# One-hot rows for eight tokens, score blocks around a staging buffer, weights two units per transfer

## The chip, the cores and the metric

The kernel runs on one core of a Trainium2 chip. The metric is the device time of one execution in microseconds (us), as the median of several runs. The engines are TensorE (PE; its weight loads are PEld), VectorE (DVE), ScalarE (ACT), GpSimd (POOL) and SyncE (SP), which only issues transfers here. Transfers are issued by SyncE, ScalarE and GpSimd and run on 16 DMA engines.

## What is computed

One decoder layer for 512 tokens of width 2048: latent attention (8 heads) and a recurrent branch side by side, an output projection, and a product-key expert layer. The last takes most of the time: 16384 experts, of which each token uses 128 (8 heads, 16 each).

```python
def chunk(xc):
    q = (xc @ w_q).reshape(TOKEN_CHUNK, N_PEER_HEADS, 2, PEER_HALF)
    s1 = jnp.einsum('chd,hnd->chn', q[:, :, 0], keys1)
    s2 = jnp.einsum('chd,hnd->chn', q[:, :, 1], keys2)
    v1, i1 = lax.top_k(s1, PEER_TOPK)
    v2, i2 = lax.top_k(s2, PEER_TOPK)
    ...
    e = i1[...] * N_KEYS + i2[...]
    g = jax.nn.softmax(top, axis=-1)
    act = gelu(einsum('chk,cd->chk', u_tab[e], xc))
    return jnp.einsum('chk,chkd->cd', g * act, v_tab[e])
```

## The kernel before

**Experts, dense and gathered.** For 384 of the 512 tokens the kernel doesn't gather: it multiplies the tokens with all 16384 expert rows, in 128 score blocks (S, 128 experts each), applies GELU, multiplies with a gate that is zero for experts not chosen, and multiplies with the value table in 128 output jobs (V). For the other 128 tokens it gathers rows: `gather` (L803) issues an indirect transfer of 1 MB on GpSimd's queue, `side` (L813) works on one gathered row with VectorE, 256 times in all.

**Weights.** Every matrix product of weights is made of three (`mm3`, L160), with each float32 operand split into a high and a low part. The weights come in units of 128x1024 (512 KB), in one fixed `order` (L77 to L103) of 631 units. `emit_next` (L117) takes the next unit: it picks a pool with fewer than two units in use, issues the transfer into `raw` (L126, two buffers per pool) on SyncE, and has ScalarE make `hi` (L130) and VectorE `lo` (L131), two buffers each. `need` (L135) gives back the unit used last and calls `emit_next` until no pool has room. A pool `base` is always open; a second one is open beside it in the input projections, the second half of the output projection and the expert layer (`open_extra`, L146), and not in the attention stage between.

**The gate stage.** When the top-k is done, the gates have to be made for 384 tokens. `onehots` (L839) builds, for four tokens at a time, one-hot rows in bf16 on VectorE: two comparisons (L847, L848) and three products with the gate's three bf16 parts (L850), three buffers of the results. `gate_mm` (L855) multiplies them on TensorE into one PSUM bank (12 products, L863), ScalarE copies the bank into `stg` (L865), which has one buffer for 32 tokens, and after eight calls the store to `GD` (L868) is issued on ScalarE's queue, 2 MB. Between the calls `park` (L665) computes score blocks ahead of their turn: two units of `ud`, 48 products, a GELU on ScalarE (L674) and a store to `AD`. 44 blocks are parked in all, 10 of them in the top-k before, 32 in the loop at L872, 2 after it (L880).

```python
    for q in range(NB4):
        if q % 3 == 0:
            park()
            if q % 6 == 3 or q > 42:
                side(rowp)
        if q + 2 < NB4:
            onehots(q + 2)
        gate_mm(q)
    while parked[0] < PARK:
        park()
```

**The main loop** (L937) runs the other 84 score blocks and the 128 output jobs. It needs two units per job, loads gates for four blocks at a time with `gates` (L893, from `GD`), multiplies them in `gated` (L900), and runs `side` at a fixed rate per unit.

**What sets the order.** PSUM has eight banks; `bank()` (L60) hands them out in turn before the main loop, which has two for S and six for V. Up to L889 a planner orders each engine's instructions when the kernel is built, by their place in the source, their dependencies and its own estimates of their durations, so an engine's queue need not stand as written. From L890 on (`manual_schedule`) each engine runs in the order of the source. Each queue works in order: an instruction that waits holds up what stands behind it, SyncE's transfers included.

## Time and profile before

| what | value |
|---|---|
| median of 3 runs | 3113.37 us (3109.54 to 3116.7) |
| the profiled execution | 3107.04 us, its span 3104.9 us |
| granted TensorE clock, mean | 0.986 |
| TensorE busy | 3043.2 us |
| VectorE / ScalarE / GpSimd busy | 2284.7 / 1096.5 / 393.9 us |
| moved by DMA | 691.13 MB, 223 GB/s |

The profile is of one execution. Times within it are us from the first instruction of the span. An engine's busy time counts its instructions from start to end; those of TensorE overlap one another, so the distance between starts tells more than the duration of one. The granted clock is the share of the full clock (2.4 GHz) that TensorE was given. An idle time is put down to the instruction or transfer whose end released the next one.

### The profile page before, as it was taken

What the parts mean: (1) busy time and instruction counts of PE and PEld (TensorE: products, weight loads), DVE (VectorE), ACT (ScalarE), POOL (GpSimd) and SP (SyncE); (2) the same over time, 40 slices, a digit from 0 to 9 for tenths busy, and PEclk for the clock granted to TensorE, in tenths of its full rate; (3) what the DMA queues carried; (4) which work ended last, traced back from release to release, by engine and by line L of the source; (5) the groups of instructions that cost most, each with busy time, mean ns of one, the idle gap of its engine ahead of it and who ended that gap; (6) DMA issues with size and microseconds to landing.
All of it is one profiled execution on the core that took longest, in us unless ns stands there. A gap on an engine that the chain in (4) does not pass through costs nothing.

```text
span 3104.9 us, 39324 instructions
## 1 busy us (share of the span) xinstructions
PE 3043.2 (98%) x15443; PEld 2630.8 (85%) x15443; DVE 2284.7 (74%) x3456; ACT 1096.5 (35%) x1371; POOL 393.9 (13%) x280
## 2 busy tenths in 40 slices
PE   8999999999999999999999999999999999999999
PEld 7777565678899998999999999999999999888887
DVE  4465544448999888757777777777777777788887
ACT  4455332342234444443333333333333333333332
POOL 0000000000000011001212112122211212211111
PEclk9999898999999999999999999999999999999999
DMA  7222211232245887678787787877878778878876
GB/s 247 87 78 75 88 55 41 88 108 83 89 129 195 269 274 255 200 264 290 278 296 284 283 301 274 299 284 281 296 281 296 285 282 292 298 277 295 290 283 234
DMA packets 247306, 691.13 MB, mean 223 GB/s; under 512 B 17040, under 2 KB 128272, under 8 KB 213456
## 3 DMA queue, kind: packets, MB, share of 16 engines
q1 hardware_dynamic: 152832, 382.15, 36.8%
q0 software_dynamic: 37008, 269.50, 23.2%
q10 hardware_dynamic: 57280, 36.97, 3.9%
q8 instruction: 121, 1.98, 0.3%
q14 instruction: 65, 0.53, 0.0%
HBM read 650.40 MB, written 38.14 MB: 222 GB/s over the span
## 4 chain that ended last, share of the span: by engine, by line
PE 57%; issue 0%; DVE 0%; ACT 0%
PE pV L984 11%; PE pV L983 11%; PE pV L982 11%; PE pS L161 8%; PE pS L163 8%; PE pS L162 8%; PE ps L161 0%; PE ps L162 0%; PE ps L163 0%; PE ps L863 0%; DVE acc L996 0%; ACT pact L674 0%; DVE o L850 0%; ACT hi L130 0%
## 5 line engine op out<-in xcount | busy, mean ns | idle before, releaser
L130 ACT ACTIVATE hi<-raw 128x1024 fp32r<-128x1024 f32 x631 | 667.8, 1061 | 1489.4 <-PE pS L162 487.6
L131 DVE TENSOR_TENSOR lo<-raw,hi 128x1024 fp32r<-128x1024 f32 x631 | 771.1, 1222 | 495.2 <-ACT hi L130 481.6
L161 PE MATMUL pS<-FH,hi 128*128 128x384 f32 x1344 | 449.9, 335 | 1.3 <-ACT pact L674 1.3
L163 PE MATMUL pS<-FH,lo 128*128 128x384 f32 x1344 | 450.0, 335 | 0.0
L162 PE MATMUL pS<-FL,hi 128*128 128x384 f32 x1344 | 449.5, 334 | 0.0
L984 PE MATMUL pV<-hi,FL 128*128 128x512 f32 x960 | 374.7, 390 | 0.0
L983 PE MATMUL pV<-lo,FH 128*128 128x512 f32 x960 | 374.7, 390 | 0.0
L982 PE MATMUL pV<-hi,FH 128*128 128x512 f32 x960 | 373.4, 389 | 0.0
L161 PE MATMUL ps<-FH,hi 128*128 128x384 f32 (+1 forms) x960 | 342.8, 357 | 0.3 <-ACT hi L130 0.3
L809 POOL DMA_INDIRECT row<-in_un,E x128 | 175.6, 1372 | 1319.3 <-DVE row L821 819.3
L163 PE MATMUL ps<-FH,lo 128*128 128x384 f32 (+1 forms) x960 | 337.8, 352 | 0.6 <-DVE lo L131 0.6
L162 PE MATMUL ps<-FL,hi 128*128 128x384 f32 (+1 forms) x960 | 338.1, 352 | 0.0
L821 DVE SCALAR_TENSOR_TENSOR row<-row,xg 128x2048 f32<-128x2048 f32 x128 | 292.5, 2285 | 22.0 <-DMA row<-in_un,E 22.0
L826 DVE SCALAR_TENSOR_TENSOR acc<-row,W,acc 128x2048 f32<-128x2048 f32 x128 | 300.2, 2345 | 0.0
L809 POOL DMA_INDIRECT row<-in_vn,E x128 | 192.4, 1503 | 804.8 <-DVE acc L826 754.0
L161 PEld LDWEIGHTS pS<-FH,hi 128*128 128x128 f32 x1344 | 252.3, 188 | 4.7 <-ACT pact L674 1.7
L162 PEld LDWEIGHTS pS<-FL,hi 128*128 128x128 f32 x1344 | 252.3, 188 | 3.1
L163 PEld LDWEIGHTS pS<-FH,lo 128*128 128x128 f32 x1344 | 252.2, 188 | 0.0
L996 DVE TENSOR_TENSOR acc<-pV,acc 128x512 f32<-128x512 f32 x384 | 240.9, 682 | 8.3 <-PE pV L984 8.3
L984 PE MATMUL pV<-hi,pl 128*128 128x512 f32 x576 | 224.4, 390 | 0.0
L983 PE MATMUL pV<-lo,ph 128*128 128x512 f32 x576 | 224.2, 389 | 0.0
L982 PE MATMUL pV<-hi,ph 128*128 128x512 f32 x576 | 224.0, 389 | 0.0
(281 smaller groups left out, 4423.2 us busy)
## 6 DMA issues: line engine op xcount, KB each, us to landing
raw<-in_ud SPq DMA_DIRECT2D x256, 512.0 KB
raw<-in_vd SPq DMA_DIRECT2D x256, 512.0 KB
G<-GD SPq DMA_DIRECT2D x33, 768.0 KB
GD<-stg ACTq DMA_DIRECT2D x12, 2048.0 KB
raw<-in_win SPq DMA_DIRECT2D x44, 512.0 KB
raw<-in_wo SPq DMA_DIRECT2D x32, 512.0 KB
raw<-in_wq SPq DMA_DIRECT2D x32, 512.0 KB
AD<-pact ACTq DMA_DIRECT2D x44, 192.0 KB
```

The source lines that it names most:

```text
L130: s.activation(hi, raw, AF.Copy)
L131: v.tensor_tensor(lo, raw, hi.bitcast(F32), op=OP.subtract)
L161: pe.matmul(out, ah, bh, start=start, stop=False)
L162: pe.matmul(out, ah, bl, start=False, stop=False)
L163: pe.matmul(out, al, bh, start=False, stop=stop)
L809: g.indirect_dma_start(out=r, out_offset=None, in_=d["un" if j < 128 else "vn"], in_offset=bass.IndirectOffsetOnAxis(ap=E0[:, j % 128:j % ...
L821: v.scalar_tensor_tensor(r, r, 1.0, xg, op0=OP.mult, op1=OP.mult, accum_out=dots[:, j:j + 1])
L826: v.scalar_tensor_tensor(acc[:, 0, :], r, W0[:, j - 128:j - 127], acc[:, 0, :], op0=OP.mult, op1=OP.add)
L982: pe.matmul(pss[t], ph[:, t, :], hi[:, cs], start=pr + bj == 0, stop=False)
L983: pe.matmul(pss[t], ph[:, t, :], lo[:, cs], start=False, stop=False)
L984: pe.matmul(pss[t], pl[:, t, :], hi[:, cs], start=False, stop=pr + bj == 2)
L996: v.tensor_tensor(a, pss[t], a, op=OP.add)
```

## The change

It has four parts. The one-hot rows are built for eight tokens at a time, in half as many instructions of twice the length, with two buffers instead of three; one comparison is written into the third of the product rows, so its own buffer is gone. The loop of the gate stage has 48 steps of eight tokens; a score block is parked in three of every four steps, not in the fourth, at whose end the staging buffer is stored, and `side` runs in every second step. The weights are moved by `bring`, two units in one transfer of 1 MB into one buffer of 128x2048 per pool (the first two units, `wkr`, `wv`, `wuq` and `wuk` alone, 512 KB each), and split by `split`, one unit at a time; the tables are laid out so that both units of a pair stand in one row of 8 KB per partition. `ones`, `identb` and `maskb` move to a pool that is closed after the output projection.

```diff
-    ones = cp.tile([128, 128], F32, name="ones")
-    v.memset(ones, 1.0)
-    identb = cp.tile([128, 128], BF, name="identb")
-    maskb = cp.tile([128, 128], BF, name="maskb")
...
-    order = []
+
+    groups = []
     for m in range(6):
-        order += [("win", m, 0), ("win", m, 1)]
-    order.append(("wkr",))
+        if m == 0:
+            groups += [([("win", 0, u)], d["win"][0][:, u]) for u in range(2)]
+        else:
+            groups.append(([("win", m, 0), ("win", m, 1)], d["win"][m]))
+    groups.append(([("wkr",)], d["wkr"]))
...
     for hb in range(2):
-        order += [("wv", hb)] + [("wuq", hb, u) for u in range(3)] + [("wuk", hb)]
-        order += [("wo", dc, 4 + u) for dc in (2 * hb, 2 * hb + 1) for u in range(4)]
...
+        groups.append(([("wv", hb)], d["wv"][hb]))
+        groups += [([("wuq", hb, u)], d["wuq"][hb, u]) for u in range(3)]
+        groups.append(([("wuk", hb)], d["wuk"][hb]))
+        groups += wo_pairs(2 * hb, 4) + wo_pairs(2 * hb + 1, 4)
...
+    groups += [([("wq", m, 0), ("wq", m, 1)], d["wq"][m]) for m in range(16)]
...
         if j[0] == "S":
-            order += [("ud", j[1], 0), ("ud", j[1], 1)]
+            groups.append(([("ud", j[1], 0), ("ud", j[1], 1)], d["ud"][j[1]]))
         else:
-            order += [("vd", j[1], j[2], 0), ("vd", j[1], j[2], 1)]
+            groups.append(([("vd", j[1], j[2], 0), ("vd", j[1], j[2], 1)], d["vd"][j[1], j[2]]))
+    order = [k for keys, _ in groups for k in keys]
     pools = [base]
-    live = {id(base): 0}
+    live, busy = {id(base): 0}, {id(base): False}
     limit = [0]
+    moved, raws = [0, 0], []
     ready, nxt, used, last = {}, [0], [0], [None]
...
-    def emit_next():
+    def bring():
+
+        if moved[0] >= len(groups):
+            return False
+        keys, src = groups[moved[0]]
+        ps = pools if moved[1] + len(keys) <= limit[0] else pools[:1]
+        ps = [p for p in ps if not busy[id(p)]]
+        if not ps:
+            return False
+        p = ps[0]
+        moved[0] += 1
+        moved[1] += len(keys)
+        busy[id(p)] = True
+        raw = p.tile([128, 2048], F32, name="raw", bufs=1)[:, :len(keys) * 1024]
+        sy.dma_start(raw, src if len(keys) == 1 else src.rearrange("p u c -> p (u c)"))
+        raws.append([raw, p, len(keys), 0])
+        return True
+
+    def split():
+
         ps = pools if nxt[0] < limit[0] else pools[:1]
         ps = [p for p in ps if live[id(p)] < 2]
-        if nxt[0] >= len(order) or not ps:
+        if not raws or not ps:
             return False
-        key = order[nxt[0]]
-        nxt[0] += 1
+        r = raws[0]
+        raw = r[0][:, r[3] * 1024:(r[3] + 1) * 1024]
+        r[3] += 1
         p = min(ps, key=lambda p: live[id(p)])
         live[id(p)] += 1
-        raw = p.tile([128, 1024], F32, name="raw", bufs=2)
-        sy.dma_start(raw, unit_src(key))
         hi = p.tile([128, 1024], F32R, name="hi", bufs=2)
         lo = p.tile([128, 1024], F32R, name="lo", bufs=2)
         s.activation(hi, raw, AF.Copy)
         v.tensor_tensor(lo, raw, hi.bitcast(F32), op=OP.subtract)
-        ready[key] = (hi, lo, p)
+        ready[order[nxt[0]]] = (hi, lo, p)
+        nxt[0] += 1
+        if r[3] == r[2]:
+            raws.pop(0)
+            busy[id(r[1])] = False
         return True
+
+    def emit_next():
+        a = bring()
+        return split() or a
...
     sqB = MBp.tile([128, S], F32, name="sqB")
+    ones = MBp.tile([128, 128], F32, name="ones")
+    v.memset(ones, 1.0)
+    identb = MBp.tile([128, 128], BF, name="identb")
+    maskb = MBp.tile([128, 128], BF, name="maskb")
...
-    NT = 4
-    NB4 = TD // NT
+    NT = 8
+    NB8 = TD // NT
...
-        o2 = gp.tile([128, NT, 64, 2], BF, name="o2", bufs=3)
-        o1 = gp.tile([128, NT, 64, 2], BF, name="o1", bufs=1)
-        o3 = gp.tile([128, 3, NT, 64, 2], BF, name="o3", bufs=3)
+        o2 = gp.tile([128, NT, 64, 2], BF, name="o2", bufs=2)
+        o3 = gp.tile([128, 3, NT, 64, 2], BF, name="o3", bufs=2)
...
-        v.tensor_tensor(o1, io, e1T[:, c, None].to_broadcast(sh), op=OP.is_equal)
+        v.tensor_tensor(o3[:, 2], io, e1T[:, c, None].to_broadcast(sh), op=OP.is_equal)
         for j in range(3):
-            v.tensor_tensor(o3[:, j], o1, g3T[:, j, c, None].to_broadcast(sh), op=OP.mult)
+            v.tensor_tensor(o3[:, j], o3[:, 2], g3T[:, j, c, None].to_broadcast(sh), op=OP.mult)
...
     def gate_mm(q):
-
         o2, o1 = oh.pop(q)
-        if q % 8 == 0:
+        if q % 4 == 0:
             stg[0] = gp.tile([128, 128, 32], F32, name="stg", bufs=1)
...
+        for hf in range(2):
+            ps = bank()
+            for i in range(4):
+                for j in range(3):
+                    pe.matmul(ps[:, i * 128:(i + 1) * 128], o2[:, 4 * hf + i], o1[:, j, 4 * hf + i],
+                              start=j == 0, stop=j == 2)
+            c = (q % 4) * 8 + hf * 4
+            s.activation(stg[0][:, :, c:c + 4].rearrange("p a t -> p t a"),
+                         ps.rearrange("p (t a) -> p t a", t=4), AF.Copy)
+        if q % 4 == 3:
+            s.dma_start(GD[q // 4].rearrange("g p x -> p g x"), stg[0].rearrange("p (g a) t -> p g (a t)", a=GRP))
+
+    onehots(0)
+    for q in range(NB8):
+        if q % 4 != 3:
             park()
-            if q % 6 == 3 or q > 42:
-                side(rowp)
-        if q + 2 < NB4:
-            onehots(q + 2)
+        if q % 2 == 1:
+            side(rowp)
+        if q + 1 < NB8:
+            onehots(q + 1)
         gate_mm(q)
...
-    o["ud"] = c(o["un"].reshape(128, 128, 2, 8, 128).transpose(0, 2, 4, 3, 1)).reshape(128, 2, 128, 1024)
-    o["vd"] = c(o["vn"].reshape(32, 2, 2, 128, 4, 512).transpose(0, 4, 1, 3, 2, 5)).reshape(32, 4, 2, 128, 1024)
+    o["ud"] = c(o["un"].reshape(128, 128, 2, 8, 128).transpose(0, 4, 2, 3, 1)).reshape(128, 128, 2, 1024)
+    o["vd"] = c(o["vn"].reshape(32, 2, 2, 128, 4, 512).transpose(0, 4, 3, 1, 2, 5)).reshape(32, 4, 128, 2, 1024)
```

## Rows read from the trace of the kernel before

**Rows 1.** The page, part 1: busy us (share of the span) and instructions.

```profile
PE 3043.2 (98%) x15443; PEld 2630.8 (85%) x15443; DVE 2284.7 (74%) x3456; ACT 1096.5 (35%) x1371; POOL 393.9 (13%) x280
```

**Rows 2.** By stage: us, PE, PEld, DVE, ACT, POOL busy, clock, DMA, GB/s.

```profile
0.00:50.00 50.00, 41.05 (x166) 32.59 (x167) 26.83 (x58) 29.43 (x41) 0.43 (x5) 1.00 0.88 303
...
255.00:590.00 335.00, 324.45 (x1209) 202.89 (x1207) 169.35 (x287) 126.45 (x214) 14.91 (x11) 0.93 0.21 65
...
962.00:1351.00 389.00, 363.15 (x2789) 354.51 (x2788) 303.24 (x604) 178.10 (x203) 31.81 (x26) 0.97 0.74 242
1351.00:3105.00 1754.00, 1748.78 (x8640) 1565.46 (x8640) 1381.20 (x1398) 541.79 (x633) 336.79 (x231) 1.00 0.80 286
```

**Rows 3.** TensorE in order of time, gate stage: start, us, instruction [idle before <-releaser].

```profile
962.21 0.42 PE L161 MATMUL ps<-FH,hi 128*128 128x384 f32 x1
...
1123.13 0.42 PE L161 MATMUL ps<-FH,hi 128*128 128x384 f32 x1
...
1131.54 0.23 PE L863 MATMUL ps<-o,o 128*128 128x128 bf16 x1
...
1133.54 0.42 PE L161 MATMUL ps<-FH,hi 128*128 128x384 f32 x1
...
1148.74 0.27 PE L863 MATMUL ps<-o,o 128*128 128x128 bf16 x1 [5.28 <-ACT stg L865]
...
1150.30 0.67 PE L161 MATMUL ps<-FH,hi 128*128 128x384 f32 x1
...
1350.85 0.44 PE L161 MATMUL pS<-FH,hi 128*128 128x384 f32 x1 [1.35 <-ACT pact L674]
```

**Rows 4.** ScalarE in order of time, one store of the staging buffer.

```profile
1123.62 0.38 ACTq L868 DMA_DIRECT2D GD<-stg  x1
...
1139.43 2.10 ACT L865 ACTIVATE stg<-ps 128x512 f32<-128x512 f32 x2 [10.97 <-DMA GD<-stg]
```

**Rows 5.** The waits of all engines: us in total, times, longest us.

```profile
ACT stg L865 <- DMA GD<-stg: 61.7, 11, 11.0
...
DVE row L821 <- DMA row<-in_un,E: 22.0, 14, 3.8
...
PE ps L863 <- ACT stg L865: 12.3, 3, 5.3
...
PE ps L863 <- DVE o L850: 11.4, 4, 4.3
```

**Rows 6.** Ten us of the gate stage (columns of rows 2).

```profile
1240.00:1250.00 10.00, 6.46 (x29) 6.20 (x30) 9.73 (x22) 5.29 (x7) 0.00 (x0) 0.66 0.83 275
```

**Rows 7.** The costliest groups, shapes apart: xcount | busy us, mean ns.

```profile
L131 DVE TENSOR_TENSOR lo<-raw,hi 128x1024 fp32r<-128x1024 f32 x631 | 771.1, 1222 | 495.2 <-ACT hi L130 481.6 <-PE ps L691 8.4 <-PE ps L228 4.2
...
L821 DVE SCALAR_TENSOR_TENSOR row<-row,xg 128x2048 f32<-128x2048 f32 x128 | 292.5, 2285 | 22.0 <-DMA row<-in_un,E 22.0
...
L850 DVE TENSOR_TENSOR o<-o,g3T 128x512 bf16<-128x512 bf16 x288 | 105.1, 420 | 0.4
...
L776 DVE TENSOR_TENSOR eq<-eq 128x1024 bf16<-128x1024 bf16 x8 | 5.5, 683 | 0.0
```

**Rows 8.** The waits of SyncE's queue.

```profile
SPq L895 <- DMA GD<-stg: 11.7, 1, 11.7
```

**Rows 9.** Gathers (line 809), then the raw weights from 1400 us on.

```profile
DMA to landing us min/median/max: 5.4/7.3/10.7
...
  DMA raw<-in_vd: 12.3, 10
```

**Rows 10.** ScalarE in order of time, two units of the attention stage.

```profile
460.09 1.06 ACT L130 ACTIVATE hi<-raw 128x1024 fp32r<-128x1024 f32 x1 [2.30 <-PE ps L162]
...
467.90 1.06 ACT L130 ACTIVATE hi<-raw 128x1024 fp32r<-128x1024 f32 x1 [2.29 <-PE ps L162]
```

**Rows 11.** The start, in order of time: SyncE's queue, VectorE.

```profile
2.60 0.44 SPq L127 DMA_DIRECT2D raw<-in_win  x1
...
8.15 1.22 DVE L131 TENSOR_TENSOR lo<-raw,hi 128x1024 fp32r<-128x1024 f32 x1
```

More of the change, by code (lines that the diff above doesn't have):

```diff
@@ L66, in body, with wo_pairs @@
     ident = cst[:, K_ID:K_ID + 128]
-    ones = cp.tile([128, 128], F32, name="ones")
-    v.memset(ones, 1.0)
-    identb = cp.tile([128, 128], BF, name="identb")
-    maskb = cp.tile([128, 128], BF, name="maskb")
     def col(c):
         return vec[:, c:c + 1]
-    order = []
+    groups = []
     for m in range(6):
-        order += [("win", m, 0), ("win", m, 1)]
-    order.append(("wkr",))
+        if m == 0:
[3 more added lines that the diff above has]
+    groups.append(([("wkr",)], d["wkr"]))
     for h in range(8):
-        order += [("win", 6 + h, 0), ("win", 6 + h, 1), ("win", 14 + h, 0), ("win", 14 + h, 1)]
+        groups += [([("win", m, 0), ("win", m, 1)], d["win"][m]) for m in (6 + h, 14 + h)]
+    def wo_pairs(dc, lo_):
+        return [([("wo", dc, u), ("wo", dc, u + 1)], d["wo"][dc, u // 2]) for u in (lo_, lo_ + 2)]
     for hb in range(2):
-        order += [("wv", hb)] + [("wuq", hb, u) for u in range(3)] + [("wuk", hb)]
-        order += [("wo", dc, 4 + u) for dc in (2 * hb, 2 * hb + 1) for u in range(4)]
-    order += [("wo", dc, u) for dc in range(4) for u in range(4)]
-    order += [("wq", m, 0, u) for m in range(16) for u in range(2)]
-    order = [(k[0], k[1], k[3]) if k[0] == "wq" else k for k in order]
+        groups.append(([("wv", hb)], d["wv"][hb]))
+        groups += [([("wuq", hb, u)], d["wuq"][hb, u]) for u in range(3)]
+        groups.append(([("wuk", hb)], d["wuk"][hb]))
+        groups += wo_pairs(2 * hb, 4) + wo_pairs(2 * hb + 1, 4)
+    for dc in range(4):
+        groups += wo_pairs(dc, 0)
+    groups += [([("wq", m, 0), ("wq", m, 1)], d["wq"][m]) for m in range(16)]
     JOBS = [("S", b) for b in range(PARK)]
@@ L148, in open_extra @@
         pools.append(p)
-        live[id(p)] = 0
+        live[id(p)], busy[id(p)] = 0, False
         limit[0] = order.index(until) if until else len(order)
@@ L154, in close_extra @@
         pools.remove(p)
-        assert all(r[2] is not p for r in ready.values())
+        assert all(r[2] is not p for r in ready.values()) and all(r[1] is not p for r in raws)
         if last[0] is p:
@@ L857, in gate_mm @@
         o2, o1 = oh.pop(q)
-        if q % 8 == 0:
+        if q % 4 == 0:
             stg[0] = gp.tile([128, 128, 32], F32, name="stg", bufs=1)
-        ps = bank()
-        for i in range(4):
-            for j in range(3):
-                pe.matmul(ps[:, i * 128:(i + 1) * 128], o2[:, i], o1[:, j, i], start=j == 0, stop=j == 2)
-        qq = q % 8
-        s.activation(stg[0][:, :, qq * 4:(qq + 1) * 4].rearrange("p a t -> p t a"),
-                     ps.rearrange("p (t a) -> p t a", t=4), AF.Copy)
-        if qq == 7:
-            s.dma_start(GD[q // 8].rearrange("g p x -> p g x"), stg[0].rearrange("p (g a) t -> p g (a t)", a=GRP))
-    for q in range(2):
-        onehots(q)
-    for q in range(NB4):
-        if q % 3 == 0:
+        for hf in range(2):
[12 more added lines that the diff above has]
+        if q % 4 != 3:
             park()
-            if q % 6 == 3 or q > 42:
-                side(rowp)
-        if q + 2 < NB4:
-            onehots(q + 2)
+        if q % 2 == 1:
+            side(rowp)
+        if q + 1 < NB8:
+            onehots(q + 1)
         gate_mm(q)
@@ L1032, in layout @@
     o["wg"] = c(wg.reshape(4, 4, 128, 128).transpose(2, 0, 1, 3))
-    o["wo"] = c(a["w_out"][0].reshape(8, 2, 128, 4, 512).transpose(3, 0, 2, 1, 4)).reshape(4, 8, 128, 1024)
+    o["wo"] = c(a["w_out"][0].reshape(8, 2, 128, 4, 512).transpose(3, 0, 2, 1, 4).reshape(4, 4, 2, 128, 1024).transpose(0, 1, 3, 2, 4))
     o["wq"] = c(a["peer_w_q"][0].reshape(2, 8, 128, 16, 128).transpose(3, 2, 0, 1, 4)).reshape(16, 128, 2, 1024)
```

7 lines of the change are left out of this document (removed).

## The prediction

> **What bounds the kernel now.** I read the page's busy shares first, then the same by stage, then TensorE's own order of time in the one stage that stands out, and last what its gaps wait for. TensorE is busy 98% of the span [rows 1], so only time in which it stands still, or runs at its lower clock, can be won; the change adds and removes no matrix product. The table by stage says where such time is [rows 2]. From 1351 us on it is 1748.8 busy of 1754: nothing to win there, only to lose. The gate stage, 962 to 1351, has 25.9 us of idle time and a granted clock of 0.97; the attention stage 10.6 us at 0.93, in small products that the change leaves alone; the first 50 us have 9, before anything has landed.
>
> In the gate stage the order of time shows one repeating step [rows 3]: a score block of 48 products (1123.13 to 1131.54, 8.41 us) and then the gate products of three sets of four tokens, 36 of them in 2.00 us, so 0.056 us each; 10.41 us in all. The stage has 34 blocks and 1152 gate products (384 tokens, three each): 34 x 8.41 + 1152 x 0.056 = 350 us, where 1350.85 - 962.21 = 388.6 were taken. 38.6 us are lost. One step shows how: it begins at 1133.54 and the next at 1150.30, 16.76 us instead of 10.41, with a gap of 5.28 us that ScalarE's copy into the staging buffer ends. That copy stood still because the buffer was still being written out: the store went out at 1123.62 and the next copy began at 1139.43, after 10.97 us of waiting [rows 4], and the splits of the weights (hi) stand behind it on ScalarE. In all ScalarE waits 61.7 us for the store, eleven times; TensorE's gaps are put down to the copies (12.3 us) and to the one-hot rows (11.4 us) [rows 5], and the latter are late for the same cause, since on VectorE they stand behind a split (lo) that needs hi. After a gap the clock falls: 0.66 granted in 1240 to 1250, so of its two levels, 1.2 and 2.4 GHz, it had the lower for a part of that time [rows 6]. This is why 38.6 us are lost where 25.9 are idle.
>
> **The change part by part.** *Score blocks around the staging buffer.* The 350 us of products stay. Now each run of 32 tokens is block, 8 tokens, block, 8 tokens, block, 16 tokens, and then the store. So behind every store there is a block, 24 gate products (1.3 us) and a second block before a third bank pair is wanted: at least 18.1 us of products whose weights are split already or are split before the copy that waits. The store seen took 15.8 us from issue to next copy [rows 4]. The first copy is due a block and half a set (9.1) after the last set's products, the store itself goes out about a copy (1.0) after them, so ScalarE waits 15.8 - 8.1 = 7.7 us where it waited 11, and the splits held up behind it are for a block that starts only at 18. In PSUM two 2-bank sets and two score banks fill 6 of the 8 banks by then. So I take the gaps as gone, except for what is unknown: a slow gather (VectorE stood 22.0 us on rows in fourteen places [rows 5]) or another order of the engine queues than the source has, since a planner sets it there. Bounds 0 and 15 us (0.4 of what is lost now); I take 4, near the lower end because the margin exceeds the store shown.
>
> *One-hot rows for eight tokens.* 96 x 5 instructions of 512 columns become 48 x 5 of 1024. The rows: 420 ns for 512, 683 ns for 1024 columns of the same type [rows 7]. 480 x 0.42 = 202 us become 240 x 0.683 = 164, 38 us less on VectorE. It is worth nothing directly, as VectorE is 303 of 389 busy [rows 2]; it is cover. But a batch now takes 5 x 0.683 = 3.4 us and only two are held, so batch q+1 can start only when the products of q-1 are done. While blocks stand between the products (8.41 us) that is hidden: 3.4 us + two lo splits of 1.22 + half a side step (2.29) = 7.0 us. Between the two sets that follow one another at the end of 32 tokens the second batch was made during the block. The row says so far: hidden. A rule stands against it: the Trainium skill, Perfetto Trace Analysis, section Optimizing Scalar/DVE Operations, says that where Vector isn't saturated and causes bubbles elsewhere, instructions should be broken up, not merged. By it the batch would be waited for once in every 32 tokens; that is the first rival below. The trace agrees in so far as VectorE isn't saturated and 11.4 us of bubbles bear its name [rows 5].
>
> *The tail of the stage.* 34 blocks are used up in the twelfth run, so the last three sets have no block beside them, and the two blocks that followed the last products are gone as cover. There batch 46 waits for products 44 and takes 3.4 us less 1.5 covered by products 45: 1.9 us idle, and the same for 47: 3.8. Then the main loop's first block needs banks that the last copies free. These wait for the eleventh store, then take about 1 us each [rows 4], eight of them: 0 to 7 us more. I take 6 in all (bounds 3.8 and 11). SyncE waited 11.7 us for the last store before it could load the gates [rows 8]; that load and the raw transfers behind it on SyncE's queue are late by as much now, but two blocks split and two landed, 33 us of products, lie in front of them. VectorE stands at the first gate multiply for it; three split units (12.5 us) cover that.
>
> So the stage takes 350 + 4 + 6 = 360: 28.6 us less.
>
> *Two units per transfer, one buffer per pool.* 512 KB x 2 buffers become 1 MB x 1; 618 of the 631 units go in pairs. SyncE issues half as many; it isn't waited for. What changes is that a transfer may start only when both halves of the one before are split. In the main loop a pool has 16.6 us for two jobs (84 blocks and 128 output jobs fill 1749 us); less one unit between the two splits (4.15) and hi and lo (2.3), a transfer may take 10.2 us, and 13.2 us before it sets the pace, the lead used up. The nearest row is a gather of 1 MB: 5.4 / 7.3 / 10.7 us; splits waited on raw weights for 12.3 us in all [rows 9]. I take 0. In the attention stage only one pool is open: a unit there lasts 7.81 us (460.09 to 467.90 [rows 10]), hi, lo and a median gather's 7.3 make 9.6, with one split unit in hand: between 0 and 1.8 us on ten single transfers; I take 1 in sum, since 512 KB at a DMA share of 0.21 [rows 2] must be quicker than 1 MB at 0.80. At the start, unit 1's transfer went out at 2.60; now it takes the base buffer after unit 0 and so waits until lo of unit 0 ends, 8.15 + 1.22 = 9.4 [rows 11]: 6.8 us later, and on SyncE input tiles may stand behind it. The DMA engines are 0.88 busy then, so part of this is merely another order. Bounds 0 and 6.8; I take 3.
>
> *ones, identb, maskb* move to a pool closed early; the memset and copies are the same: 0.
>
> **Sum.** -28.6 + 1 + 3 = -24.6 us. The profiled execution took 3107.0 us (span 3104.9); with the change 3082.4. The median of the runs shown is 6.3 higher, 3113.4, so I forecast **3089 us**.
>
> **Rivals.** (1) *One-hot batches become the wait.* If VectorE, with lo splits and a side step in front, delivers one batch per 32 tokens late by half to all of itself, 12 x 1.7 = 20 or 12 x 3.4 = 41 us come back. The half, which is where the trace's 78% of VectorE points: 3089 + 18 = 3107 us. For: only two batches are held, where three were. Against: the 8.41 us blocks. Chance 0.16. (2) *The stalls stay*, because the planner puts the copies ahead of the splits again or the store lengthens: with 1 MB loads and gathers beside it in 512-byte pieces it need only grow from 15.8 to some 20 us. Then the gain is a few us and the start gives it back: about 3112. Chance 0.11. (3) *Slower: one raw buffer per pool sets the main loop's pace.* It decides when a 1 MB load takes over 13.2 us from issue to landing, in the stage where DMA is 0.80 busy; each us beyond costs 106 pairs of jobs 106 us. It needs 13.4 us to cancel the gain and at 13.5 gives 3089 + 32 = 3121. For: two gathers and the gates run beside it, and the 2 MB store took up to 15.8. Against: no gather took over 10.7. Chance 0.11. The forecast keeps 0.62.
>
> A measurement of this kernel can tell about 0.2%, 6.2 us. Faster than 3107.1: 0.62, half of rival 1 and a little of rival 2, 0.72. Within: 0.16. Slower: 0.12. The low end is a stage of 350 + 3.8 with nothing lost elsewhere: 3113.4 - 34.8, 3078.6, taken down to 3077. Upward I go past rival 1 to 3111, which leaves out rival 3 and most of rival 2, about 0.2.
>
> **What would show it.** Right: the step from block to block in the gate stage is even, no gap over 2 us on TensorE before its last 20 us, ScalarE's wait for the store about 11 x 8 us or less with no gap of TensorE behind it; the main loop's first product near 1322 + 3; the main loop still 1749 us. Wrong: gaps put down to the one-hot rows in every run of 32 tokens (rival 1), gaps put down to the copies (rival 2), hi waiting for raw in the main loop and TensorE under 1.00 busy there (rival 3), or a first product later by more than 7 us.

## The result, and the profile after

The changed kernel took 3129.45 us (median of 5 runs, 3126.38 to 3131.24), the kernel before 3111.06 in the same comparison: a ratio of 1.0055, 95% interval 1.004 to 1.0069. It is slower, where 3089 was forecast. The profiled execution has a span of 3129.1 us.

The page's part 1 and the table by stage of the kernel after answer to [rows 1] and [rows 2]:

```profile
PE 3048.4 (97%) x15443; PEld 2636.6 (84%) x15443; DVE 2267.0 (72%) x3216; ACT 1099.3 (35%) x1371; POOL 396.3 (13%) x280
```

```profile
0.00:50.00 50.00, 34.83 (x122) 26.07 (x123) 25.11 (x56) 22.11 (x31) 0.43 (x5) 0.90 0.70 237
966.00:1375.00 409.00, 370.26 (x2792) 360.31 (x2791) 286.08 (x365) 181.01 (x203) 30.69 (x25) 0.95 0.69 228
1375.00:3129.00 1754.00, 1748.70 (x8640) 1565.38 (x8639) 1381.89 (x1397) 542.00 (x633) 340.00 (x232) 1.00 0.79 287
```

The main loop is what it was, 1754 us. The start has 6.2 us less of TensorE (34.83 against 41.05). The gate stage has 38.7 us in which TensorE stands still, against 25.9, although VectorE has 17 us less to do in it. TensorE in order of time shows the stage's ends and its longest gap (columns of [rows 3]):

```profile
966.62 0.42 PE L187 MATMUL ps<-FH,hi 128*128 128x384 f32 x1
...
1374.74 0.45 PE L187 MATMUL pS<-FH,hi 128*128 128x384 f32 x1 [1.11 <-ACT stg L895]
```

The stage begins 4.4 us later and takes 408.1 us, where 388.6 were taken before and 360 were forecast. The waits of all engines (answering to [rows 5]) name what holds it up:

```profile
DVE row L851 <- DMA row<-in_un,E: 75.7, 25, 8.6
...
ACT stg L895 <- DMA GD<-stg: 41.1, 10, 7.8
...
PE ps L892 <- DVE o L879: 37.5, 29, 6.0
```

ScalarE's wait for the store fell from 61.7 to 41.1 us, and inside the stage no gap of TensorE ends with a copy any more. But VectorE now waits 75.7 us for gathered rows (22.0 before; 72.4 and 19.9 of them in the stage), and TensorE 37.5 us for one-hot rows (11.4 before), in six of the twelve runs of 32 tokens and at the end. One such place, all engines in order of time, other rows left out:

```profile
1020.88 2.29 DVE L851 SCALAR_TENSOR_TENSOR row<-row,xg 128x2048 f32<-128x2048 f32 x1 [0.50 <-DMA row<-in_un,E]
...
1023.45 1.68 POOL L839 DMA_INDIRECT row<-in_un,E  x1 [7.07 <-DVE row L851]
...
1025.23 1.51 PE L892 MATMUL ps<-o,o 128*128 128x128 bf16 x24
...
1026.57 0.68 DVE L877 TENSOR_TENSOR o<-iox,e1T 128x1024 bf16<-128x1024 bf16 x1
...
1029.80 2.29 DVE L851 SCALAR_TENSOR_TENSOR row<-row,xg 128x2048 f32<-128x2048 f32 x1 [2.55 <-DMA row<-in_un,E]
...
1032.02 1.29 DVE L879 TENSOR_TENSOR o<-o,g3T 128x1024 bf16<-128x1024 bf16 x2
...
1032.77 0.29 PE L892 MATMUL ps<-o,o 128*128 128x128 bf16 x1 [6.02 <-DVE o L879]
```

It is read from the bottom. TensorE stood 6.02 us for the first product with the gate (L879) of a batch. VectorE had made that batch's two comparisons by 1027.25, and then the next instruction in its queue was a side step whose row was still under way. There is one buffer for rows, so its gather was issued only at 1023.45, after the side step of 1020.88, and landed 6.35 us later. Waiting 2.55 us and working 2.29 us on the row, VectorE held up the three products behind it. Such a round, gather and side step, takes 8.9 us here, and the planner had put the next side step right behind what could be done meanwhile, so that each round was waited for; the last of the 24 side steps ended at 1216.8 us. From 1220 us to the last 9 us TensorE had no gap, 30.56 us for each 32 tokens. Six of the 24 waits are 5.7 to 8.6 us long, 42.3 us together: their gathers went out within 3 us behind a store and were 11 to 14 us under way. TensorE's gaps in the batches right behind these six are 9.5 us in sum; the other gaps follow shorter waits, as the one shown does.

### The profile page after: what moved, and what is told of

Same layout as the page of the kernel before. It is cut to its first block, busy times and chain, and to the rows that moved or that the text cites. A ratio compares the mean times of both kernels' runs of the same rounds, so it can differ in the third digit from the quotient of the medians.

```text
span 3129.1 us, 38205 instructions
## 1 busy us (share of the span) xinstructions
PE 3048.4 (97%) x15443; PEld 2636.6 (84%) x15443; DVE 2267.0 (72%) x3216; ACT 1099.3 (35%) x1371; POOL 396.3 (13%) x280
## 3 DMA queue, kind: packets, MB, share of 16 engines
q0 software_dynamic: 37008, 269.50, 24.2%
## 4 chain that ended last, share of the span: by engine, by line
PE 89%; issue 5%; DVE 3%; DMA 1%; ACT 1%; POOL 1%; SPq 0%; POOLq 0%; ACTq 0%; DVEq 0%
PE pV L1012 11%; PE pV L1013 11%; PE pV L1011 11%; PE pS L187 7%; PE pS L189 7%; PE pS L188 7%; PE ps L187 7%; PE ps L189 7%; PE ps L188 7%; PE ps L417 2%; PE ps L419 2%; PE ps L418 2%; PE ps L892 1%; PE ps L576 1%; PE ps L575 1%
## 5 line engine op out<-in xcount | busy, mean ns | idle before, releaser
L851 DVE SCALAR_TENSOR_TENSOR row<-row,xg 128x2048 f32<-128x2048 f32 x128 | 292.5, 2285 | 75.7 <-DMA row<-in_un,E 75.7
```

What stands on the lines that cost most here:

```text
L851: v.scalar_tensor_tensor(r, r, 1.0, xg, op0=OP.mult, op1=OP.mult, accum_out=dots[:, j:j + 1])
```

## The experiments

Three theories were set against one another: (A) VectorE's waits for gathered rows make the one-hot rows late; (B) batches of eight tokens in two buffers are late by themselves; (C) the transfers of 1 MB are at fault. In the table the stage is counted from the first score block of its loop to the main loop's first product, as 962.21 to 1350.85 before, in the one execution that was profiled (e10's took 5 us more than its median, e19's 5 us less). Ratios are to the kernel before on the same chip; its medians there were 3107.4 to 3111.1 us.

| kernel | placement | one-hot buffers x tokens | transfers | side steps in the stage | stage us | median us | ratio, 95% interval |
|---|---|---|---|---|---|---|---|
| before | old | 3 x 4 | single | 24 | 388.6 | 3111.1 | 1 |
| after | new | 2 x 8 | paired | 24 | 408.1 | 3129.5 | 1.0055 (1.004 to 1.0069) |
| e1 | old | 3 x 4 | paired | 24 | 406.3 | 3130.9 | 1.0078 (1.006 to 1.0096) |
| e2 | new | 2 x 8 | single | 24 | 399.8 | 3127.5 | 1.0063 (1.0046 to 1.008) |
| e18 | new | 3 x 4 | single | 24 | 392.5 | 3118.0 | 1.0028 (1.0014 to 1.0042) |
| e16 | new | 3 x 4 | paired | 24 | 387.2 | 3106.4 | 0.9991 (0.9977 to 1.0004) |
| e4 | new | 4 x 4 | paired | 24 | 368.5 | 3089.6 | 0.9948 (0.9931 to 0.9965) |
| e15 | old | 4 x 4 | single | 24 | 374.5 | 3091.3 | 0.9945 (0.9927 to 0.9962) |
| e19 | old | 4 x 4 | paired | 24 | 375.7 | 3101.1 | 0.9975 (0.9965 to 0.9984) |
| e9 | old | 3 x 4 | single | none | 356.3 | 3078.4 | 0.9906 (0.9884 to 0.9928) |
| e10 | old | 3 x 4 | paired | none | 359.3 | 3083.8 | 0.9919 (0.9897 to 0.9941) |
| e3 | new | 2 x 8 | paired | none | 355.9 | 3082.5 | 0.9923 (0.9906 to 0.994) |
| e11 | new | 2 x 8 | paired, other pool | none | 355.9 | 3076.8 | 0.9905 (0.9884 to 0.9926) |

**Parts of the change (e1, e2).** e1 is the changed kernel with the gate stage of before; e2 is the kernel before with the gate stage of after. From the edit of e1, against the kernel after:

```diff
-    NT = 8
-    NB8 = TD // NT
+    NT = 4
+    NB4 = TD // NT
...
-        if q % 4 != 3:
...
+    for q in range(NB4):
+        if q % 3 == 0:
             park()
-        if q % 2 == 1:
-            side(rowp)
...
+            if q % 6 == 3 or q > 42:
+                side(rowp)
```

> The changed kernel with the gate stage of before (one-hot rows for four tokens, blocks every third step), so of the change only the two units per transfer and the one raw buffer per pool are left. The changed trace reached the gate stage 4.4 us later than the one before. Theory A (side steps that wait for gathered rows hold the one-hot products up on VectorE) and theory B (batches of eight tokens with two buffers are simply late) both say: 4 us over before, 3115, with a gate stage of some 389 us. Theory C (the 1 MB transfers themselves slow the gathers and the store in the gate stage) says: most of the 18 us are here, 3125 or more, with rows waited for as long as in the changed kernel (76 us).

> The kernel before with the gate stage of the change (eight tokens, blocks around the store, constants moved), weights one unit per transfer with two buffers as before. Theories A and B: a gate stage as long as in the changed kernel (408 us against 389), so 3111 + 20 = 3131, a few us either way. Theory C: a gate stage of 370 or less, 3095.

Each part alone is as slow as both together, so their costs don't add. e2 came out near what theories A and B said: without paired transfers the new stage is nearly as slow, so that theory C does not explain the whole change. e1 was a surprise: it took the time of theory C, with a stage of 406.3 us, but without that theory's sign, since rows are waited for only 12.1 us there. Its store takes a median of 15.0 us to land, and ScalarE waits 87.6 us for it (61.7 before). Three gaps of TensorE, 14.0 us, end with a copy, and seven, 22.2 us, with one-hot rows. All engines in order of time show how the store reaches the latter:

```profile
1101.53 0.38 ACTq L898 DMA_DIRECT2D GD<-stg  x1
...
1119.14 1.05 ACT L895 ACTIVATE stg<-ps 128x512 f32<-128x512 f32 x1 [9.59 <-DMA GD<-stg]
...
1122.92 2.00 ACT L148 ACTIVATE hi<-raw 128x1024 fp32r<-128x1024 f32 x2
...
1124.02 1.23 DVE L149 TENSOR_TENSOR lo<-raw,hi 128x1024 fp32r<-128x1024 f32 x1 [6.61 <-ACT hi L148]
...
1125.16 1.09 DVE L880 TENSOR_TENSOR o<-o,g3T 128x512 bf16<-128x512 bf16 x3
...
1125.63 1.57 PE L893 MATMUL ps<-o,o 128*128 128x128 bf16 x9 [5.24 <-DVE o L880]
```

ScalarE waits for the store before a copy, `hi` stands behind the copies, `lo` waits for `hi` on VectorE, the one-hot products stand behind `lo`. So two waits of different origin, for the store and for a row, end in the same place: VectorE comes late to the one-hot rows.

**No side steps in the stage (e3, e9, e10).** The 24 side steps are done in the main loop instead, at a higher rate; e3 is made from the kernel after, e9 from before, e10 from e1. The edit of e3:

```diff
-        if q % 2 == 1:
-            side(rowp)
...
-    RATE = 0.585
+    RATE = 0.65
```

> The changed kernel without the 24 side steps in the gate stage; they are done in the main loop, whose rate per unit goes from 0.585 to 0.65. Theory A: the gate stage has no gap but at its end, 350 + 9 = 360 us, 48 less, and if the main loop hides 22 more side steps 3129 - 48 = 3081. Theory B: the gate products still wait for the rows of eight tokens, stage 395 or more, 3115 to 3129.

> The kernel before with no side steps in the gate stage (its 24 are done in the main loop at a rate of 0.65 instead of 0.585). It tells what the placement of the blocks is worth when no side step is in the way. If the prediction's account of the stage before was right (TensorE's waits for ScalarE's store are the block order's own, 14 us of gaps and the clock after them; its waits for one-hot rows are the side steps'), the gaps behind the store stay and the others go: 3093 to 3102, so 11 to 20 us slower than the changed kernel without side steps (3082). Rival (all of the stalls came by way of the side steps, and the new placement is worth nothing): 3080 to 3085.

> The kernel before with the paired transfers alone, and no side steps in the gate stage (rate 0.65 in the main loop). With side steps the paired transfers alone cost 20 us, 17 of them in the gate stage, where the store took 15 us to land. If the paired transfers by themselves make the store late (1 MB loads beside it): store 14 us or more, waits for it over 60 us, and 8 us or more slower than the kernel before without side steps. Rival (the store was late because of the gathers beside it, or because the side steps fell elsewhere in the order): within 4 us of the kernel before without side steps plus the start's 3 us.

e3 came out as theory A had it, 3082.5 us. e9 came out at 3078.4, just under its rival's range: the old placement without side steps has the same stage as the new one, 356.3 against 355.9 us. e10 came out as its rival had it, 5.4 us behind e9, 3.1 of them in the stage. The waits of e9, of 960 to 1380 us, and two stretches, its stage and its main loop:

```profile
ACT stg L865 <- DMA GD<-stg: 56.5, 11, 7.9
...
PE ps L863 <- DVE o L850: 2.1, 3, 1.3
```

```profile
962.00:1318.00 356.00, 352.07 (x2786) 344.80 (x2784) 251.33 (x556) 177.86 (x203) 2.71 (x2) 1.00 0.63 193
1318.00:3076.00 1758.00, 1748.93 (x8640) 1565.62 (x8640) 1433.99 (x1446) 542.38 (x634) 379.45 (x255) 1.00 0.83 300
```

ScalarE waits for the store nearly as long as before (56.5 against 61.7 us), yet TensorE is 352 of 356 us busy, at a clock of 1.00. So most of the 38.6 us can be had with the store's wait as it is. One thing e9 leaves open: without gathers its store is also back sooner, 11.3 to 13.7 us from issue to next copy where it was 10.8 to 15.8 before, and the four longer gaps that stand behind a store there (2.7 to 5.3 us) follow stores of 14.8 to 15.8 us. e4 and e15 below close this: there the store is later than before, with side steps in the stage, and TensorE stands still less. The wait for the store is harmless as long as VectorE is ahead with its one-hot rows. The side steps took that lead, and their cost was 32.3 us of stage before and 52.2 after, while the main loop takes them for 4 to 5 us (its length is 1757.9 us in e9 and 1759.6 in e3, against 1754.0 before).

**What of a side step costs (e7, e13, e17, e14).** In e7 (from after), e13 (before) and e17 (e1) the 24 side steps all work on the first gathered row; 23 gathers and their part of the result are left out. In e14 (from after) they work on a block that is there anyway, and the gathers go on. The edit of e7:

```diff
-        r = rows.pop(j)
+        r = rows.pop(j) if j == 0 or j > 23 else rows[0]
+        if j == 0:
+            rows[0] = r
...
-        gather(*pools)
+        if j >= 23:
+            gather(*pools)
+        else:
+            ng[0] += 1
```

> The changed kernel, in which the first 24 side steps all work on the row that was gathered first: VectorE does the same 24 multiplications of 2.3 us in the gate stage, but no side step waits for a gather (23 gathers are left out, and with them their part of the result). Theory A (VectorE stands before each side step until its row has come, and the one-hot products behind it are late): the 72.4 us of waits for rows go, TensorE's waits for one-hot rows go with them, the gate stage is about 360 us instead of 408, and the time is 3080 to 3090. Rival (the 24 x 2.3 us of VectorE's own work between two 8-token batches are enough to make them late): TensorE still waits 20 to 37 us for one-hot rows, and the time is 3105 to 3130.

> The kernel before, in which the first 24 side steps all work on the row that was gathered first (23 gathers and their part of the result are left out). Without any side steps in the stage it takes 3078.4, with them 3110. Theory A (in this kernel too the waits for rows, 20 to 22 us of VectorE, make the stalls, those behind the store among them): 3078 to 3088. Rival (there VectorE's 24 x 2.3 us of own work or the order of the store make them): 3095 to 3110.

> The kernel before with the paired transfers alone, its first 24 side steps without gathers of their own (23 gathers and their part of the result are left out). With gathers it took 3130.9, without side steps 3083.8; the kernel before with such side steps 3092.7. If the gathers beside 1 MB loads make the store late (15 us to land) and through ScalarE's wait the halves and the one-hot rows: 3090 to 3100, the store back at 7 to 10 us. Rival (the 1 MB loads alone delay the store while side steps are there): 3110 to 3130, the store still over 12 us.

> The changed kernel with all 24 gathers in the gate stage, but its side steps multiply a block that is already on the chip, so that they wait for no gather (the gathered rows are not read and their part of the result is left out; a gather waits only for the one before it, so the 24 run one behind another early in the stage). Theory A (VectorE's wait for the row makes the stalls): as without gathers, 3083 to 3092. Rival (the gathers' traffic on the 16 DMA engines delays loads of weights and the store): stalls in the first 150 us of the stage, where the gathers run, waits of ScalarE for the store or for raw tiles, 3100 to 3125.

Measured: e7 3087.2 us (0.9931, 0.991 to 0.9953), stage 366.8; e13 3092.7 (0.9956, 0.9942 to 0.997), stage 378.1; e17 3107.7 (0.9996, 0.9982 to 1.0011), stage 386.5; e14 3101.3 (0.9973, 0.9961 to 0.9986), stage 372.9. After the change, then, gathers and the waits for them cost 408.1 - 366.8 = 41.3 us of stage and VectorE's own work 366.8 - 355.9 = 10.9; before it was 10.5 and 21.9. The shares hold for the order that each kernel has: with no row to wait for, the planner set the side steps closer together, and in e7 the last one ends at 1113 us instead of 1217. Theory A's waits are the larger part in the kernel after; in the one before the 24 x 2.3 us of work are, and e13 missed the range of both sides. In e7 TensorE's wait in the stage is down to this:

```profile
PE ps L897 <- DVE o L884: 8.8, 9, 2.3
```

e14 is 14 us behind e7, in its rival's range. In its trace the planner has put the side steps, which wait for nothing now, ahead, 13 of them among the top-k's work (they run from 695 to 1023 us): the stage begins 6.6 us later than in e7, and one gap of 7.87 us at 987.56 stands for its 6.0 us more of stage. So the gathers' traffic without the waits seems to cost little, though how little isn't told from the other order.

The traffic does delay the store. In e14 the stores that are issued while the 24 gathers run are 16.4 to 20.6 us from issue to next copy, those after them 9.0 to 10.4; in the kernel after 14.3 to 15.5 (one 9.8), then 8.9 to 10.4; in e3, with no gathers in the stage, 8.8 to 11.0 throughout. ScalarE waits 63.7 us for the store in e14, 33.6 in e7, and no gap of TensorE in the stage ends with a copy in either. Pairing the transfers delays it less: the median from issue to next copy goes from 11.7 to 12.6 us without side steps (e9, e10), from 11.7 to 12.9 with side steps but no gathers (e13, e17), from 12.6 to 15.3 with gathers (before, e1). e17, at 3107.7, lies under its rival's range and over the other: even without gathers pairing costs 12 us beside e13 by the ratios, 8.4 of them in the stage. What makes up these 8.4 us was not settled.

**Where the side steps stand (e8, e12).** e8 keeps the stage in the order of the source. e12 has four-token rows in two buffers, and two buffers for gathered rows. From the edit of e8:

```diff
+    ctx = tc.manual_schedule()
+    ctx.__enter__()
     onehots(0)
     for q in range(NB8):
```

> The changed kernel with the gate stage's instructions kept in the order in which the program is written, so that a side step stands at every second batch of 8 tokens (about 15.3 us apart) and not where the planner puts it (8.2 to 8.9 us apart in the first 250 us). Theory A: a row has 15 us for a round of about 10 us (gather and multiplication), so that VectorE finds it there; waits for rows under 10 us in the stage, the stage 355 to 370 us, the time 3080 to 3095. Rival (VectorE's own work in the batch is what makes it late, wherever the side step stands): no better than 3110. If the written order is worse than the planner's in other ways (the halves of the units, GELU and the store on ScalarE), blocks of products will show gaps that wait for hi or lo.

> The changed placement with one-hot rows for four tokens (as in the run that gave 3089.6), but two buffers of them instead of four, and in the room so gained a second buffer for gathered rows, so that a gather is under way while VectorE works on the row before. Theory A (a single row buffer: each gather starts only when the side step before is done, and the planner sets the side steps closer than that round takes): waits for rows under 10 us in the stage, the time 3080 to 3087. Rival (it is the reserve of one-hot rows that counts, or the traffic of the gathers): with two buffers instead of four TensorE waits more for one-hot rows, 3095 to 3125.

Both forecasts of theory A failed: 3126.7 us (1.0061, 1.0038 to 1.0084), a stage of 402.0, and 3155.6 (1.0148, 1.0126 to 1.0171), a stage of 434.7; e12 is beyond its rival's range too. The waits of e8, of 960 to 1400 us:

```profile
DVE lo L149 <- ACT hi L148: 116.3, 24, 10.7
ACT stg L895 <- DMA GD<-stg: 76.6, 11, 8.6
...
PE ps L892 <- DVE o L879: 30.7, 35, 2.8
...
DVE row L851 <- DMA row<-in_un,E: 3.4, 1, 3.4
```

The rows are there in time, as forecast (the one wait of 3.4 us is in the main loop), and TensorE still waits 30.7 us for one-hot rows, because now the other chain makes VectorE late: store, `hi`, `lo`. At 1017.95, for one, `lo` has waited 10.71 us for a `hi` that stood behind copies, and these had waited 8.63 us for the store. (ScalarE also waits 26.1 us for raw tiles in that stage, which was not told apart.) In e12 the waits for rows are 16.3 us (22.7 in e4, which has the same placement and four-token rows), while TensorE's waits for one-hot rows rose (14.0 in e4):

```profile
PE ps L893 <- DVE o L880: 54.0, 37, 7.9
...
DVE row L851 <- DMA row<-in_un,E: 16.3, 5, 5.3
```

Taking away the wait for rows does not help if the reserve of one-hot rows goes with it. e12's gathers also follow one another more closely, and its store is up to 20.6 us under way; the runs don't tell that apart from the reserve, and a second row buffer beside the full reserve was not run.

**The reserve (e4, e15, e16, e19) and the placement (e18).** In these the number of four-token buffers is three or four, in both placements. From e16 to e4 it is the number alone that changes. With the fourth buffer e15 and e19 also build a batch further ahead, and they, like e18, write the comparison into the product rows as the change does. From the edit of e15:

```diff
-        o2 = gp.tile([128, NT, 64, 2], BF, name="o2", bufs=3)
+        o2 = gp.tile([128, NT, 64, 2], BF, name="o2", bufs=4)
...
-    for q in range(2):
+    for q in range(3):
         onehots(q)
```

> The changed kernel with one-hot rows for four tokens at a time in four buffers (the same memory), blocks and side steps placed as in the change. Theory B: the gaps go, stage 360 to 370, about 3085. Theory A: the side steps stand in the same places and wait for the same rows, the stage stays at 395 to 410, 3118 to 3130.

> The kernel before with four buffers of one-hot rows for four tokens instead of three (the identity and mask tiles moved to make the room); the placement of the blocks, the side steps and the transfers are as before. The changed kernel with such rows in four buffers took 3089.6, and 3082.5 without side steps. Theory R (the reserve of one-hot rows in front of TensorE decides what the side steps cost): the stage falls from 389 to about 368 us as there, the time to 3082 to 3092. Theory P (the new placement, with the products of several batches between two blocks, is what the rest of the gain came from): 3100 to 3112, as before.

> The changed kernel with one-hot rows for four tokens in three buffers, as the kernel before has them; with four it took 3089.6. Theory R (reserve): the stage rises from 368 to 385 to 405 us, the time to 3105 to 3125. Theory P (placement) or batch size alone: 3088 to 3095.

> The kernel before with the new placement of blocks around the staging buffer alone: one-hot rows for four tokens in three buffers and single transfers, as before, and the side steps in the stage. The prediction gave the placement 28.6 us. Without side steps it is worth nothing (356.3 and 355.9 us of stage). If it is worth something where side steps make the splits late: 3085 to 3100. If it only mends what the paired transfers do (3130.9 with them in the old placement, 3106.4 in the new): 3104 to 3112, as before.

> The old placement with paired transfers (3130.9) and four buffers of one-hot rows for four tokens instead of three. If the reserve of one-hot rows covers whatever makes VectorE late (as it did without pairing, 3107.7 to 3091.3), the pairing's price in the stage falls to a few us and the start's 5 stay: 3095 to 3103. If the pairing's price is another one (splits late for their raw tiles, ScalarE behind a store of 15 us): 3110 to 3125.

By the ratios one more buffer takes 13, 17 and 32 us off in three kernels: e16 to e4, before to e15, e1 to e19. e4 and the kernel after hold the same bytes of one-hot rows, 4 x 4 and 2 x 8 tokens, and differ by 33 us by the ratios, 39.6 in the stage. That is what theory B had said, but not batch size alone: in e4 the planner also sets the side steps 10 to 13 us apart instead of mostly 8.2 to 9.4, and rows are waited for 22.7 us instead of 72.4. So neither theory holds alone: batches of eight in two buffers are harmless without the waits (e3, and nearly so e7), and with smaller batches the waits are fewer and are covered. In the median e4 has the latest store of all, 18.0 us from issue to next copy, where it was 12.6 before (waits of 960 to 1335 us):

```profile
ACT stg L895 <- DMA GD<-stg: 77.8, 10, 10.3
...
DVE row L851 <- DMA row<-in_un,E: 22.7, 8, 3.8
...
PE ps L892 <- DVE o L879: 14.0, 12, 2.4
```

In e15, with the old placement, the waits for rows and for the store are longer than before too, and TensorE's waits are shorter: 13.2 us for one-hot rows and 0.7 for copies, where they were 11.4 and 12.3 (waits of 960 to 1380 us):

```profile
ACT stg L864 <- DMA GD<-stg: 86.9, 11, 10.5
...
DVE row L821 <- DMA row<-in_un,E: 36.2, 14, 5.8
...
PE ps L862 <- DVE o L849: 13.2, 15, 2.8
```

The placement alone (e18) is slower than before. As the prediction had it, no gap inside its stage ends with a copy; but TensorE's waits for one-hot rows rise to 24.2 us, the stage is 3.9 us longer, and the main loop 10.0, with a gap near its start (in e2 too, 5.08 us) that the prediction had seen and thought covered. ScalarE's longest wait of 1350 to 1400 us, and TensorE there:

```profile
ACT hi L126 <- DMA raw<-in_ud: 21.9, 2, 18.6
```

```profile
1375.98 0.69 PE L157 MATMUL pS<-FH,hi 128*128 128x384 f32 x1 [5.48 <-ACT pact L960]
```

On SyncE's queue the next units stand behind the load of the gates, which waits for the last store. With paired transfers, as in the change, two more units lie in front, and the gap isn't there: for the change itself the prediction was right about it. Beside paired transfers the placement is worth something: e1 to e16 is 27 us by the ratios. That it does so by shielding the stage from a late store, which the kernel before needed less, fits the 14.0 us behind copies in e1 and 1.1 in e16, but was not shown apart.

**The start (e11).** From e3, with another choice of the pool.

```diff
-        p = ps[0]
+        p = min(ps, key=lambda p: live[id(p)])
```

> The changed kernel without side steps in the gate stage (3082.5), in which a transfer goes to the pool with the fewest units in use instead of to the first pool that is free. If the start's loss of some 4 us comes from the choice of the pool (the second raw tile of a pair waits although another pool is empty): TensorE's busy time in the first 50 us goes from 35 back to 39 to 41 us, the time to 3077 to 3080, as the kernel before without side steps (3078.4). Rival (the loss is that of the larger transfer itself, which lands later): no change, 3081 to 3084.

The first 50 us of e3, then of e11:

```profile
0.00:50.00 50.00, 34.98 (x124) 26.43 (x125) 25.21 (x56) 22.13 (x31) 0.43 (x5) 0.90 0.72 241
```

```profile
0.00:50.00 50.00, 38.73 (x153) 29.67 (x154) 25.91 (x57) 25.00 (x35) 0.43 (x5) 1.00 0.80 272
```

TensorE gets 3.7 us back, and the median falls from 3082.5 to 3076.8; the forecast was 39 to 41 us of TensorE in this stretch, against 38.7, and 3077 to 3080. e11 and e9 beat both kernels, by about 1% each; between them there is nothing to tell apart. Of all that was tried, moving the side steps out of the stage gains most; on top of it the change's parts are worth nothing that can be told.

## Why the prediction was wrong

The stage was forecast at 360 us and took 408.1. One gap of the kernel before, in two rows, VectorE and then TensorE:

```profile
973.02 2.29 DVE L821 SCALAR_TENSOR_TENSOR row<-row,xg 128x2048 f32<-128x2048 f32 x1 [1.73 <-DMA row<-in_un,E]
...
976.44 0.26 PE L863 MATMUL ps<-o,o 128*128 128x128 bf16 x1 [4.29 <-DVE o L850]
```

- **The step that failed first: "38.6 us are lost" to the staging buffer.** The prediction followed the gaps back to the store, and put those behind one-hot rows down to "the same cause". For the longest of these four gaps, 4.29 us of the 11.4, that is misread. It stands before the first store, which is issued at 1001.1 us, and VectorE was in a side step (the two rows above). For the others the chain was read rightly, but what ended a wait last is not what it would take to end it: e9 leaves the source of the store and of the placement as they were, and the stage falls by 32.3 us; e4 and e15 have later stores and smaller gaps. The loss belonged to the side steps, which the prediction had only as half a step's work in a sum that came out as "hidden". The placement, forecast at -28.6 us together with its batches, is worth 0.4 us of stage without side steps (e9, e3) and costs time alone (e18).
- **The second: "hidden" for the batches of eight.** 3.4 + two splits + half a side step = 7.0 us against a block of 8.41 counted VectorE's work and none of its waits. The waits for gathered rows were in a term of 4 us, bounds 0 and 15. Measured: 408.1 - 350 = 58.1 us beyond the products, of which 4.5 are the tail's gaps (6 had been taken, and the first of them, 1.9 us, came at 1.95); 53.6 stand where 4 were taken, 41.3 of them for gathers and the waits for them (e7). The 38 us that VectorE was to save came out at 17, since instructions that follow one another on it overlap: two of 683 ns took 1.29 us from the first start to the last end in the place shown above.
- **Rival 1 named where it would show**, one-hot batches as the wait, but not why. Its upper price of 41 us gives 3089 + 41 = 3130, and that this is what was measured is luck: it counted twelve batches late by VectorE's own 3.4 us each, where TensorE waited 29 times and VectorE's own work was worth 10.9 us (e7). It got 0.16, and a price of 18 us where its own half is 12 x 1.7 = 20, because the block of 8.41 us was held to cover VectorE. The Trainium skill, Perfetto Trace Analysis, section Optimizing Scalar/DVE Operations, was cited there: where an engine isn't saturated but causes bubbles on others, breaking its instructions up may let work be done sooner. The runs agree in so far as batches of four with the same bytes are 33 us faster than batches of eight (e4), though VectorE is busy longer with them, 299.8 us of the stage against 285.5; the side steps stand elsewhere too.
- **e4 met the forecast of 3089 us**, at 3089.6, and that is luck as well: e15, with the old placement, took 3091.3.
- **Right:** the main loop at 0, so rival 3 falls (the paired loads landed in medians of 5.3 and 5.7 us); ScalarE's longest wait for the store, 7.8 us where 7.7 were reckoned, and no gap behind it in the stage.
- **Right in sum, by luck in size:** the start and the attention stage, +4 forecast, +4.4 measured. The place was named rightly (the second unit in the base pool; e11), but TensorE's hundredth product starts at 45.04 us instead of 35.05, 10.0 us late, beyond the bound of 6.8. By 600 us some 7 us are got back, in part where the kernel before has a gap of 2.38 us that a `hi` ends (589.19) and this one has none, and 1.7 are lost again after. The prediction had no term for that.
- **Rival 2** (the stalls stay by way of the store) is in part what e1 shows, 14.0 us of gaps that end with copies, not the whole change.

## What to carry to other kernels

Before moving work around a wait, ask what would cover it: take the suspected load off the engine that comes late (here the side steps off VectorE) and see whether the wait still costs anything. On an engine that works in order, an optional step that reads a transfer costs its wait as well as its work, and if a planner places it by its own estimate, closer together than one buffer allows, everything behind it pays; put such steps where the engine has a lead. For a producer with fixed room, more and smaller batches held off such waits better here than fewer and larger ones, and one buffer more of the same batches did so by itself (e16 to e4).

## What the runs showed that was not expected

- The costs of the parts don't add: by the ratios, pairing the transfers costs 24 us alone, the new gate stage 20, both together 17. They end in the same lateness of VectorE; that the new placement shields the stage from the store that pairing delays is a reading, not shown apart.
- A gap costs more than its length. In the kernel after, the score block that follows the gap of 6.02 us and two shorter ones took 9.56 us from its first start to its last end, at a granted clock of 0.89, where blocks without a gap before them took 8.58 at 1.00. So 38.7 us of idle time became 58.1 us lost. The granted clock of the stage is 0.95 there; without side steps (e9) it is 1.00, the level of 2.4 GHz throughout.
- The same wait of ScalarE for the store, 56 to 62 us, costs TensorE next to nothing in one kernel and stands in front of its longest gaps in another. How long an engine waits says little on what the wait is worth.
- Gathers and the store hold each other up when they meet: stores took mostly 14 to 15 us beside gathers and 9 to 10 after them, and the gathers right behind a store 11 to 14 us instead of 5 to 8 (kernel after).
